# Background rounding with four raw and two high tiles, and gate and up weights loaded by depth halves

## The chip, the cores and the metric

The kernel runs on one core of a Trainium2 chip. The core has a matrix engine (TensorE, PE in the profile; its weight loads are listed as PEld), a vector engine (VectorE, DVE), an activation engine (ScalarE, ACT), a general engine (GpSimd, POOL) and a queue engine (SyncE, SP) that here only issues transfers. Data moves between the chip's memory and the on-chip memory (128 partitions) in transfers over 16 DMA engines. Each engine works through its own list of instructions in order and waits on semaphores for the others; an SP entry that has to wait therefore holds up everything behind it on SP. The metric is the device time of one execution in microseconds.

## The reference

One layer of a decoder with a sequence of 1024 rows and a model width of 1024, all in float32. Only the shape of it matters here:

```python
x = x + 0.5 * swiglu(rms_norm(x, g_ffn1), w1_gate, w1_up, w1_down)   # d_ff = 2816
h = rms_norm(x, g_mix)
proj = h @ w_in          # queries, keys, values and gates of two attention branches
...                      # sparse attention (a), stick-breaking attention (b)
x = x + merged @ w_out
x = x + 0.5 * swiglu(rms_norm(x, g_ffn2), w2_gate, w2_up, w2_down)

def swiglu(h, w_gate, w_up, w_down):
    return (silu(h @ w_gate) * (h @ w_up)) @ w_down
```

The weights `w_gate` and `w_up` are 1024 by 2816, `w_down` is 2816 by 1024. `w_in` is used in the middle of the layer, long after the first FFN.

## The kernel before

**Precision.** The matrix engine takes a rounded format. To keep float32 accuracy, each operand is split into a high part (the value rounded, written by ACT) and a low part (the value minus its high part, by POOL or DVE). A product then takes three matmuls: high by high, high by low, low by high. `halve` (L375 to L379) does such a split: ACT at L377, the subtraction at L378.

**The two FFNs.** `ffn_in` computes silu(h·gate) times (h·up) for the first FFN (tile names a...) and for the second (b...). The 2816 columns go in eleven pairs of 128-column blocks, `p`, and for each pair the gate (`e` = 0) and the up weights (`e` = 1). A pair with a depth of 1024 is a two by two matrix of blocks: A11 and A12 are the two depth halves of the first column block, A21 and A22 those of the second. From the second pair on, each of these two by two products is done with seven block products instead of eight (Strassen's scheme in Winograd's form). I call seven such products a set; there are twenty in an FFN, a gate set and an up set in turn. A product is 12 matmuls (L468 to L470: three for each of four depth chunks). The first pair is done by `opening` with eight plain block products.

Inside `products` (L477) the seven run in the order 1, 6, 7, 5, 2, 4, 3. Four PSUM letters, pa to pd, hold the results. ACT reads pa after the first product (L481), and DVE adds pb, pc and pd to running sums after the second, third and fourth (L484, L488, L491). The fifth and the seventh product go on accumulating in pa and pd, so they can start only after L481 and L491. Behind L491 DVE forms the four sums of the next set (L457 to L460, kept in program order), which ACT and POOL then split, together with the plain quarters (seven `halve` calls, L461). After an up set, DVE multiplies gate by up and forms sums of the result (L612, L589 to L592), and SP stores seven tiles to memory (L594) for the second half of the FFN, `ffn_out`, which starts at L680.

**Weights of gate and up.** `loader` (L437) loads one column block of 128 columns at full depth into a tile of 1024 floats per partition: eight runs of 128 floats, 512 bytes each. Of two such tiles the left 512 columns are A11 and A21, the right ones A12 and A22.

**Background rounding.** While the first FFN runs, the kernel also splits 24 column blocks of `w_in` (16 for the gates, eight for queries and keys), for later use, into high and low parts kept in memory. Each block goes in two pieces of 128 by 512: 48 pieces. `beside` (L784) is called after every product of the first FFN with the product's place in its set, 0 to 6. A piece takes three steps: load the raw weights (SP, L799); round them into a high tile (ACT, L789) and subtract in place, which leaves the low part in the raw tile (DVE, L790); store both (SP, L793). `behind` ties a step to the last matmul of the product, so that it cannot start earlier. There are three slots, each with one raw and one high tile. Their steps stand in `points` as (split, store, load): slot 0 at places 0, 1 and 3, slot 1 at 2, 3 and 5, slot 2 at 4, 5 and, in the next set, 0. A load goes into the tiles that its slot's store has just been reading, and at place 3 the load of slot 0 is written before the store of slot 1. The six tiles come from leftover space: c3 (three), c1 (one) and pair (two).

The order of instructions on each engine is settled at build time by a scheduler that goes by a simulated timeline, except in `opening` and where `keep_in_program_order` pins it.

Of the kernel before, what the change touches and what calls it, by code (L numbers as in the profile page):

```python
# [16 lines left out]
AF = mybir.ActivationFunctionType  # L17
ALU = mybir.AluOpType
# [5 lines left out]
P = 128  # L24
# [3 lines left out]
ND = D // P  # L28
# [29 lines left out]
def f32(ap):  # L58
    return ap.bitcast(F32)
# [186 lines left out]
def trunk(ctx, tc, x, positions, g_ffn1, w1_gate, w1_up, w1_down, g_mix, w_in, g_cq, w_uq_a, w_q_idx,  # L246
          g_q_a, g_k_a, w_uv_a, w_o_a, w_o_b, w_out, g_ffn2, w2_gate, w2_up, w2_down, inv_freq, out):
    nc = tc.nc
# [63 lines left out]
    def in_turn(*sources):  # L312

        order = [f for n in range(max(n for f, n in sources)) for f, m in sources if n < m]
        at = [0]

        def tile_(name):
            at[0] += 1
            return order[(at[0] - 1) % len(order)](name)

        return tile_
# [53 lines left out]
    def halve(t, src, eng=None):  # L375

        nc.scalar.activation(t[:, HI], src, AF.Copy)  # L377
        (eng or nc.gpsimd).tensor_tensor(t[:, LO], src, f32(t[:, HI]), op=ALU.subtract)  # L378
        return t  # L379

    class Right:


# [51 lines left out]
                nc.vector.tensor_sub(out[j], a[j], b[j])  # L435

    def loader(raw, nm):  # L437
        def load(w, f, name):
            t = raw(name)
            nc.sync.dma_start(t.rearrange("p (k f) -> p k f", k=ND),  # L440
                              w[0, :, f * P:(f + 1) * P].rearrange("(k p) f -> p k f", p=P))
            return t

        return load

    def ffn_in(nm, R, wg, wu, raw, op, sums, ct, bank, staged, rows, first=None, beside=lambda n, ins: None):

# [2 lines left out]
        B, load = R.B, loader(raw, nm)  # L450

        def left_sides(rs, name, pinned):
            A11, A12, A21, A22 = (r[:, q] for r in rs for q in (HI, LO))
            O = {n: op(f"{name}{n}") for n in ("A11", "S2", "S3", "S1", "A12", "A22", "S4")}
            s1, s2, s3, s4 = (sums(f"{name}s{n}") for n in range(1, 5))
            in_turn_ = tc.keep_in_program_order if pinned else lambda i: i
            in_turn_(nc.vector.tensor_add(s1, A21, A22))  # L457
            in_turn_(nc.vector.tensor_sub(s2, s1, A11))
            in_turn_(nc.vector.tensor_sub(s3, A11, A21))
            in_turn_(nc.vector.tensor_sub(s4, A12, s2))  # L460
            for n, src in (("A11", A11), ("S2", s2), ("S3", s3), ("S1", s1), ("A12", A12), ("A22", A22), ("S4", s4)):  # L461
                halve(O[n], src)
            return O

        def times(a, b, ps, start=True):
# [35 lines left out]
        def opening(raws, rows, nxt):  # L501


            A = [dict(zip(("A11", "A12", "A21", "A22"), (r[:, q] for r in rs for q in (HI, LO)))) for rs in raws]
            O = ({}, {})

            def left(e, *names):
                for n in names:
                    O[e][n] = halve(op(f"{nm}{e}0{n}"), A[e][n])

            ps, sg = {}, {}

            def half(e, r, c, q):

                letter = "abcd"[r + 2 * c]
                if not q:
                    ps[e, r, c] = bank(f"p{letter}", letter)
                times(O[e][f"A{r + 1}{q + 1}"], B[f"B{q + 1}{c + 1}"], ps[e, r, c], not q)

            def gate(r, c):  # L520
                sg[r, c] = ct(f"{nm}sg")
                nc.scalar.activation(sg[r, c], ps[0, r, c], AF.Silu)

            def gated(r, c):
                nc.vector.tensor_mul(sg[r, c], sg[r, c], ps[1, r, c])

            if "B11" not in B:
                left(0, "A11")
                R.operand("B12")
                R.turn("B11")  # L530
                left(0, "A12")
                R.turn("B21")
                left(0, "A21", "A22")
                R.second()
            else:
                left(0, "A11", "A12", "A21", "A22")
            for t, n in enumerate(("A11", "A12", "A21", "A22")):
                if 4 - t <= len(rows):
                    R.stat(rows[t + len(rows) - 4])
                left(1, n)  # L540
            for t in rows:
                R.norm(t)
            half(0, 0, 0, 0)
            half(0, 0, 0, 1)
            gate(0, 0)
# [12 lines left out]
            half(0, 0, 1, 0)  # L558
            R.turn("T1", "ab")
            half(0, 0, 1, 1)  # L560
            gate(0, 1)
            R.sum("T2")
            half(0, 1, 1, 0)
            R.turn("T2", "ab")
            half(0, 1, 1, 1)
            gate(1, 1)
            R.sum("T4")
            R.sum("T3")
            half(1, 0, 1, 0)
            half(1, 0, 1, 1)  # L570
            R.turn("T3", "ab")
            gated(0, 1)
            nxt = nxt()
            half(1, 1, 1, 0)
            half(1, 1, 1, 1)
            R.turn("T4", "ab")
            gated(1, 1)
            return [sg[0, 0], sg[0, 1], sg[1, 0], sg[1, 1]], [ct(f"{nm}s{n}") for n in range(3)], nxt
# [17 lines left out]
        def lefts(p, e, pinned=False):  # L596
            if p == NF // 2:
                return None
            return left_sides([load((wg, wu)[e], 2 * p + q, f"{nm}{e}r{p}") for q in range(2)], f"{nm}{e}{p}", pinned)

        for p in range(NF // 2):
            if not p:
                first = first or [[load(w, q, f"{nm}{e}r0") for q in range(2)] for e, w in enumerate((wg, wu))]
                with tc.manual_schedule(engines={e.engine for e in (nc.tensor, nc.vector, nc.scalar, nc.gpsimd)}):
                    H, S, nxt = opening(first, rows, lambda: lefts(1, 0))
            else:
                for e, w in enumerate((wg, wu)):
                    u, nxt = products(nxt, f"{nm}{e}", lambda: lefts(p + e, 1 - e, True))
                    if not e:
                        H = silu(u)  # L610
                for a, b in zip(H, u):
                    nc.vector.tensor_mul(a, a, b)  # L612
                S = u[1:]
            finish(p, H, S)
# [147 lines left out]
    with tc.tile_pool(name="ring1", bufs=1) as rpool, tc.tile_pool(name="s1", bufs=1) as spool, tc.tile_pool(name="ps1", bufs=1, space=PSUM) as psum:  # L762
# [3 lines left out]
        with tc.tile_pool(name="t1", bufs=1, side="right") as tpool, tc.tile_pool(name="c1", bufs=1) as cpool:  # L766
# [2 lines left out]

            c4, c5, c3, c1 = (of(cpool, f"c{n}", n, 512, F32R) for n in (4, 5, 3, 1))  # L770
            ct = fp(in_turn(*[(f, 1) for f in [c4] * 4 + [c5] * 5]))
            spare = in_turn((c3, 3), (c1, 1), (pair, 2))
            R = Right(g_ffn1, bank, fp(op), fp(in_turn((c5, 5), (c3, 3))), tt, "a")
            xs = []

            pieces = [(nm, c) for nm in columns for c in range(0, 1024, 512)]
            held, points = {}, ((0, 1, 3), (2, 3, 5), (4, 5, 0))

            def behind(ins, *others):
                for o in others:  # L780
# [2 lines left out]

            def beside(n, ins):  # L784

                for slot, (split_, store, load_) in enumerate(points):
                    if n == split_ and slot in held:
                        nm, c, raw, hi = held[slot]
                        behind(ins, nc.scalar.activation(hi, raw, AF.Copy))  # L789
                        nc.vector.tensor_tensor(raw, raw, f32(hi), op=ALU.subtract)  # L790
                    if n == store and slot in held:
                        nm, c, raw, hi = held.pop(slot)
                        behind(ins, *(nc.sync.dma_start(d[:, c:c + 512], part)  # L793
                                      for d, part in zip(split_of[nm], (f32(hi), raw))))
                    if n == load_ and pieces:
                        nm, c = pieces.pop(0)
                        raw, hi = f32(spare(f"swr{slot}")), spare(f"swh{slot}")
                        held[slot] = nm, c, raw, hi
                        behind(ins, nc.sync.dma_start(raw.rearrange("p (k f) -> p k f", f=P),  # L799
                                                      rows_of[:, c // P:(c + 512) // P, columns[nm]:columns[nm] + P]))  # L800

            def rows(t):
                xs.append(fp(tt)(f"x{t}"))
# [3 lines left out]
            for t in range(4):  # L807
                rows(t)
                if t == 1:
                    R.gain()  # L810
            first = [[load(w, q, f"a{e}r0") for q in range(2)] for e, w in enumerate((w1_gate, w1_up))]
            for t in range(4, NT):
                rows(t)
            gcolm = column(g_mix, ND, "gcolm")
# [9 lines left out]
                R.norm(t)  # L824
            R.second = lambda: R.place(xs[4:8], 1, sums)
            ffn_in("a", R, w1_gate, w1_up, raw, op, sums, ct, bank, staged[0], range(4), first, beside)
            assert not held and not pieces
        hpool.append(tc.tile_pool(name="hpool", bufs=1, side="right"))
        hstack = ExitStack()
        hpool[0] = hstack.enter_context(hpool[0])  # L830
# [1342 lines left out]
```

## Time and profile before

| | |
|---|---|
| median of three runs | 2239.9 us (2239.87 to 2240.59) |
| the profiled execution's own time | 2240.86 us |
| its span, first to last instruction | 2239.1 us |
| mean granted TensorE clock | 0.989 |
| PE busy | 2169.2 us (97%) |
| DVE, ACT, POOL busy | 1526.3, 1104.4, 858.2 us |
| moved by DMA | 381.01 MB, 170 GB/s on average |

The page gives busy time by engine and in 40 slices, the DMA queues, the chain of work that ended last, the costliest groups of instructions and the DMA issues with their time from issue to landing. Groups are named by line, engine, operation and tiles (out<-in). A wait is written as the engine and line that waited, an arrow, and what released it. On the page the clock row is 9 (90% or more) in every slice of 56 us; shorter windows show where it fell.

### The profile page before, as it was taken

To read this page: it belongs to the slowest core of one execution; us is meant where nothing else is said; L and a number is where in the kernel's file an instruction comes from. 1 tells how busy PE (TensorE), PEld (TensorE's weight loads), DVE (VectorE), ACT (ScalarE), POOL (GpSimd) and SP (SyncE) were. 2 spreads that over 40 slices of the span, in tenths; PEclk is the share of its full clock that TensorE was granted. 3 is DMA by queue.
4 is the path that set the end of the run, shared out by engine and by line. 5 is a ranking of instruction groups with operands and counts; after the bars stand their busy time and mean duration, and the time that the engine had idled before them with its cause. 6 is when DMAs were issued, how large, how long until landed. Compare 5 with 4: busy or idle time off the path is not lost.

```text
span 2239.1 us, 30578 instructions
## 1 busy us (share of the span) xinstructions
PE 2169.2 (97%) x10460; PEld 1807.1 (81%) x10460; DVE 1526.3 (68%) x2548; ACT 1104.4 (49%) x2169; POOL 858.2 (38%) x698
## 2 busy tenths in 40 slices
PE   7999999999999999899999899999999999999999
PEld 6887787788878988788788788877888888888877
DVE  5675675687875498677788688853465564668685
ACT  4333333334445258999989466533333232233443
POOL 3355455532236344211111322255245454552233
PEclk9999999999999999999999999999999999999999
DMA  5376676688686333665554623566223233349755
GB/s 171 99 216 199 205 239 190 195 286 275 198 219 177 111 118 126 195 176 170 151 160 164 209 95 99 170 218 236 67 77 117 90 113 97 115 160 324 229 165 184
DMA packets 269052, 381.01 MB, mean 170 GB/s; under 512 B 23264, under 2 KB 157040, under 8 KB 268896
## 3 DMA queue, kind: packets, MB, share of 16 engines
q1 hardware_dynamic: 256384, 339.17, 48.9%
q0 software_dynamic: 12512, 39.89, 4.9%
q8 instruction: 82, 1.34, 0.2%
q14 instruction: 74, 0.61, 0.1%
HBM read 259.94 MB, written 119.05 MB: 169 GB/s over the span
## 4 chain that ended last, share of the span: by engine, by line
PE 70%; ACT 7%; DVE 6%; DMA 4%; issue 3%; POOL 2%; SPq 0%; ACTq 0%; POOLq 0%; DVEq 0%
PE p L681 6%; PE p L682 6%; PE p L680 6%; ACT junka L1186 3%; PE pd L468 3%; PE pd L469 3%; PE pd L470 3%; PE pc L470 3%; PE pc L468 3%; PE pc L469 3%; PE pa L469 3%; PE pa L468 3%; PE pa L470 3%; PE psf L308 2%; PE psf L309 2%
## 5 line engine op out<-in xcount | busy, mean ns | idle before, releaser
L1186 ACT ACTIVATE junka<-u,cand,sig 128x768 bf16<-128x768 f32 (+4 forms) x186 | 183.8, 988 | 5.6 <-DVE cand L1183 4.0
L790 DVE TENSOR_TENSOR swr<-swr,swh 128x512 f32<-128x512 f32 x48 | 45.8, 954 | 111.2 <-ACT swh L789 107.2
L789 ACT ACTIVATE swh<-swr 128x512 fp32r<-128x512 f32 x48 | 30.2, 630 | 165.6 <-DMA swr<-in_w_in_dram 56.5
L1627 DVE TENSOR_TENSOR_SCAN left<-left 128x640 f32<-128x640 f32 (+3 forms) x64 | 86.3, 1349 | 4.0 <-ACT left L1619 4.0
L1120 POOL DMA_DIRECT2D gd<-evg x32 | 17.9, 560 | 152.6 <-ACT evg L1117 112.7
L1676 DVE TENSOR_TENSOR pt<-pstT,pt 128x512 fp32r<-128x512 f32 (+1 forms) x96 | 50.8, 549 | 28.6 <-ACT pt L1674 28.3
L584 ACT ACTIVATE b0u<-b0u 128x512 f32<-128x512 f32 x20 | 12.7, 633 | 95.3 <-DVE b0u L491 78.9
L1676 DVE TENSOR_TENSOR pt<-pspT,pt 128x512 fp32r<-128x512 f32 x72 | 46.8, 684 | 16.3 <-ACT pt L1674 16.3
L681 PE MATMUL p<-bT,bS 128*128 128x512 f32 x132 | 52.5, 398 | 2.4 <-DVE bT L378 2.4
L1674 ACT ACTIVATE pt<-pspT 128x512 fp32r<-128x512 f32 x72 | 39.7, 596 | 29.2 <-PE pspT L1886 29.1
L1807 ACT ACTIVATE e<-e,nm 128x256 f32<-128x256 f32 (+7 forms) x64 | 49.3, 773 | 9.3 <-DVE nm L1802 9.2
L1540 DVE SCALAR_TENSOR_TENSOR u<-relu,WI,u 128x512 f32<-128x512 f32 (+1 forms) x70 | 50.1, 733 | 5.2 <-ACT relu L1533 4.6
L1795 DVE CUSTOM_DVE_ANT_0 e<-psL,bias 128x512 f32<-128x512 f32 (+3 forms) x96 | 49.7, 550 | 5.5 <-PE psL L1832 5.5
L682 PE MATMUL p<-bT,bS 128*128 128x512 f32 x132 | 51.9, 396 | 1.0 <-POOL bS L378 1.0
L681 PE MATMUL p<-aT,aS 128*128 128x512 f32 x132 | 51.5, 390 | 0.0
L1630 DVE TENSOR_TENSOR sa<-sa,left 128x639 f32<-128x639 f32 (+3 forms) x64 | 48.1, 752 | 3.7 <-ACT sa L1621 0.2
L682 PE MATMUL p<-aT,aS 128*128 128x512 f32 x132 | 50.4, 389 | 0.0
L1674 ACT ACTIVATE pt<-pstT 128x512 fp32r<-128x512 f32 (+1 forms) x96 | 47.1, 519 | 3.3 <-PE pstT L1730 3.1
L1533 ACT ACTIVATE relu<-psdot 128x512 f32<-128x512 f32 (+1 forms) x80 | 40.1, 520 | 17.4 <-DVE u L1540 8.6
L1886 PE MATMUL pspT<-ident,e 128*128 128x128 f32 x288 | 39.6, 277 | 8.1 <-DVE ri L1809 5.5
L1619 ACT ACTIVATE left<-psz 128x512 f32<-128x512 f32 (+2 forms) x96 | 46.2, 505 | 2.0 <-PE psz L1654 1.8
L1621 ACT ACTIVATE sa<-psz 128x512 f32<-128x512 f32 (+2 forms) x96 | 47.0, 511 | 0.1
(3021 smaller groups left out, 8247.8 us busy)
## 6 DMA issues: line engine op xcount, KB each, us to landing
aw<-in_w_down_dram SPq DMA_DIRECT2D x33, 512.0 KB, 4.9
bw<-in_w_down_dram SPq DMA_DIRECT2D x33, 512.0 KB, 5.0
swr<-in_w_in_dram SPq DMA_DIRECT2D x48, 256.0 KB, 5.1
a0r<-in_w_gate_dram SPq DMA_DIRECT2D x22, 512.0 KB, 6.7
a1r<-in_w_up_dram SPq DMA_DIRECT2D x22, 512.0 KB, 7.2
b0r<-in_w_gate_dram SPq DMA_DIRECT2D x22, 512.0 KB, 4.2
b1r<-in_w_up_dram SPq DMA_DIRECT2D x22, 512.0 KB, 3.9
x<-in_x_dram SPq DMA_DIRECT2D x16, 512.0 KB, 6.1
```

The source lines that it names most:

```text
L468: nc.tensor.matmul(ps, a[:, c], b[k][:, HI], start=start and k == 0, stop=False, skip_group_check=True)
L469: nc.tensor.matmul(ps, a[:, c], b[k][:, LO], start=False, stop=False, skip_group_check=True)
L470: ins = nc.tensor.matmul(ps, a[:, l], b[k][:, HI], start=False, stop=k == 3, skip_group_check=True)
L680: nc.tensor.matmul(ps[q][m], S[:, h], T[:, HI], start=p == 0, stop=False)
L681: nc.tensor.matmul(ps[q][m], S[:, h], T[:, LO], start=False, stop=False)
L682: nc.tensor.matmul(ps[q][m], S[:, l], T[:, HI], start=False, stop=p == last)
L1186: nc.scalar.activation(junks[1][:, 0:(i + 1) * P], score[i], AF.Sign, scale=sig[:, b:b + 1], bias=cand.bitcast(F32)[:, b:b + 1], accum_out ...
L1540: nc.vector.scalar_tensor_tensor(ac, r, wv, ac, op0=ALU.mult, op1=ALU.add)
L1627: nc.vector.tensor_tensor_scan(back, back, back, 1.0, op0=ALU.mult, op1=ALU.bypass)
L1674: nc.scalar.activation(pt[:, off:512], tp[:, off:512], AF.Copy)
L1676: nc.vector.tensor_sub(pt[:, 512 + off:1024], tp[:, off:512], f32(pt[:, off:512]))
L1795: nc.vector.tensor_tensor_reduce(e[:, c], lp[:, 0:n_], bias[:, c], 1.0, LOW, op0=ALU.add, op1=ALU.max, accum_out=m)
```

## The change

Two things are changed.

First, the loads of gate and up weights, in both FFNs. A tile now holds one depth half of both column blocks: four runs of 256 floats, 1 KB each, as many bytes as before. The quarters A11 to A22 become views of four runs of 128 floats, 256 apart: A11 and A21 lie in the first tile, A12 and A22 in the second. The sums (L457 to L460) and the splits of the quarters and sums work on such views; a new function `quarter` takes the place of `halve` there. The number and size of these operations stay the same.

Second, the background rounding of the first FFN. The four c3 and c1 tiles rotate as raw tiles, the two pair tiles as high tiles. Three pieces are still rounded per set, at places 0, 2 and 4, and stored at places 1, 3 and 5, from the second set on. The load of a piece is now due three products after the rounding of the piece four before it, at places 3, 5 and 0 of the next set, into that piece's raw tile, and that is six or seven products ahead of its own rounding. Where a store and a load are due at one place, the store comes first. A high tile is written again by the second rounding after.

```diff
+    def quarter(t, src):
+        nc.scalar.activation(by_depth(t[:, HI]), src, AF.Copy)
+        nc.gpsimd.tensor_tensor(by_depth(t[:, LO]), src, by_depth(f32(t[:, HI])), op=ALU.subtract)
+        return t
...
-        def load(w, f, name):
+        def load(w, p, q, name):
             t = raw(name)
-            nc.sync.dma_start(t.rearrange("p (k f) -> p k f", k=ND),
-                              w[0, :, f * P:(f + 1) * P].rearrange("(k p) f -> p k f", p=P))
+            nc.sync.dma_start(t.rearrange("p (k f) -> p k f", k=4),
+                              w[0, q * 512:q * 512 + 512, p * 2 * P:(p + 1) * 2 * P].rearrange("(k p) f -> p k f", p=P))
             return t
...
+    def quarters(rs):
+        t = [r.rearrange("p (k m f) -> p m k f", k=4, m=2) for r in rs]
+        return [t[q][:, m] for m in range(2) for q in range(2)]
+
+    def by_depth(a):
+        return a.rearrange("p (k f) -> p k f", k=4)
...
-            A11, A12, A21, A22 = (r[:, q] for r in rs for q in (HI, LO))
+            A11, A12, A21, A22 = quarters(rs)
...
-            spare = in_turn((c3, 3), (c1, 1), (pair, 2))
+            early, late = fp(in_turn((c3, 3), (c1, 1))), pair
...
-            held, points = {}, ((0, 1, 3), (2, 3, 5), (4, 5, 0))
+            splits = [7 * (k // 3 + 1) + (0, 2, 4)[k % 3] for k in range(len(pieces))]
+            agenda, held, halved, turn = defaultdict(list), [], [], [0]
+            for k, n in enumerate(splits):
+                agenda[n].append("split")
+                agenda[n + 1].append("store")
+                agenda[splits[k - 4] + 3 if k > 3 else k].append("load")
...
             def beside(n, ins):
+                at, turn[0] = turn[0], turn[0] + 1
+                for step in agenda.pop(at, ()):
+                    if step == "load":
+                        nm, c = pieces.pop(0)
+                        raw = early("swr")
+                        held.append((nm, c, raw))
+                        behind(ins, nc.sync.dma_start(raw.rearrange("p (k f) -> p k f", f=P),
+                                                      rows_of[:, c // P:(c + 512) // P, columns[nm]:columns[nm] + P]))
+                    elif step == "split":
+                        nm, c, raw = held.pop(0)
+                        hi = late("swh")
                         behind(ins, nc.scalar.activation(hi, raw, AF.Copy))
                         nc.vector.tensor_tensor(raw, raw, f32(hi), op=ALU.subtract)
+                        halved.append((nm, c, raw, hi))
+                    else:
+                        nm, c, raw, hi = halved.pop(0)
                         behind(ins, *(nc.sync.dma_start(d[:, c:c + 512], part)
                                       for d, part in zip(split_of[nm], (f32(hi), raw))))
```

More of the change, by code (lines that the diff above doesn't have):

```diff
@@ L452, in left_sides @@
         def left_sides(rs, name, pinned):
-            A11, A12, A21, A22 = (r[:, q] for r in rs for q in (HI, LO))
+            A11, A12, A21, A22 = quarters(rs)
             O = {n: op(f"{name}{n}") for n in ("A11", "S2", "S3", "S1", "A12", "A22", "S4")}
-            s1, s2, s3, s4 = (sums(f"{name}s{n}") for n in range(1, 5))
+            s1, s2, s3, s4 = (by_depth(sums(f"{name}s{n}")) for n in range(1, 5))
             in_turn_ = tc.keep_in_program_order if pinned else lambda i: i
@@ L461, in left_sides @@
             for n, src in (("A11", A11), ("S2", s2), ("S3", s3), ("S1", s1), ("A12", A12), ("A22", A22), ("S4", s4)):
-                halve(O[n], src)
+                quarter(O[n], src)
             return O
@@ L501, in opening @@
         def opening(raws, rows, nxt):
-            A = [dict(zip(("A11", "A12", "A21", "A22"), (r[:, q] for r in rs for q in (HI, LO)))) for rs in raws]
+            A = [dict(zip(("A11", "A12", "A21", "A22"), quarters(rs))) for rs in raws]
             O = ({}, {})
@@ L508, in left @@
                 for n in names:
-                    O[e][n] = halve(op(f"{nm}{e}0{n}"), A[e][n])
+                    O[e][n] = quarter(op(f"{nm}{e}0{n}"), A[e][n])
             ps, sg = {}, {}
@@ L598, in lefts @@
                 return None
-            return left_sides([load((wg, wu)[e], 2 * p + q, f"{nm}{e}r{p}") for q in range(2)], f"{nm}{e}{p}", pinned)
+            return left_sides([load((wg, wu)[e], p, q, f"{nm}{e}r{p}") for q in range(2)], f"{nm}{e}{p}", pinned)
         for p in range(NF // 2):
             if not p:
-                first = first or [[load(w, q, f"{nm}{e}r0") for q in range(2)] for e, w in enumerate((wg, wu))]
+                first = first or [[load(w, 0, q, f"{nm}{e}r0") for q in range(2)] for e, w in enumerate((wg, wu))]
                 with tc.manual_schedule(engines={e.engine for e in (nc.tensor, nc.vector, nc.scalar, nc.gpsimd)}):
@@ L784, in beside @@
             def beside(n, ins):
-                for slot, (split_, store, load_) in enumerate(points):
-                    if n == split_ and slot in held:
-                        nm, c, raw, hi = held[slot]
+                at, turn[0] = turn[0], turn[0] + 1
[9 more added lines that the diff above has]
+                        hi = late("swh")
                         behind(ins, nc.scalar.activation(hi, raw, AF.Copy))
                         nc.vector.tensor_tensor(raw, raw, f32(hi), op=ALU.subtract)
-                    if n == store and slot in held:
-                        nm, c, raw, hi = held.pop(slot)
+                        halved.append((nm, c, raw, hi))
+                    else:
+                        nm, c, raw, hi = halved.pop(0)
                         behind(ins, *(nc.sync.dma_start(d[:, c:c + 512], part)
                                       for d, part in zip(split_of[nm], (f32(hi), raw))))
[L795 to L800, printed above, removed]
             def rows(t):
@@ L810, in trunk @@
                     R.gain()
-            first = [[load(w, q, f"a{e}r0") for q in range(2)] for e, w in enumerate((w1_gate, w1_up))]
+            first = [[load(w, 0, q, f"a{e}r0") for q in range(2)] for e, w in enumerate((w1_gate, w1_up))]
             for t in range(4, NT):
@@ L826, in trunk @@
             ffn_in("a", R, w1_gate, w1_up, raw, op, sums, ct, bank, staged[0], range(4), first, beside)
-            assert not held and not pieces
+            assert not agenda and not held and not halved and not pieces
         hpool.append(tc.tile_pool(name="hpool", bufs=1, side="right"))
```

## The prediction

> **What bounds the kernel now.** I read the page first, then the busy time of two stretches that run the same matmuls, then the waits, the chain and SyncE's queue (SP) inside the slower one.
>
> The page's first rows: the span, and the busy time of TensorE (PE) with its share and instructions.
>
> ```profile
> span 2239.1 us, 30578 instructions
> PE 2169.2 (97%) x10460; PEld 1807.1 (81%) x10460; DVE 1526.3 (68%) x2548; ACT 1104.4 (49%) x2169; POOL 858.2 (38%) x698
> ```
>
> Only 70 us of the span are without a matmul, so a gain must come from a place where PE waits. The products of the first FFN (gate and up, tiles a...) and of the second (b...) are the same code. The first rows of each tile's and line's view give their starts; the windows view gives the stretches between, with busy time (and count) of each engine, then clock, DMA share and GB/s.
>
> ```profile
> L468 PE MATMUL pc<-aT,a01S x4: 389/392/478, 75.3 to 77.9; 128*128 128x512 f32 x4
> L468 PE MATMUL pc<-bT,b01S x4: 389/389/476, 1639.0 to 1641.6; 128*128 128x512 f32 x4
> L680 PE MATMUL p<-aT,aS x132: 388/389/395, 478.4 to 654.9; 128*128 128x512 f32 x132
> L680 PE MATMUL p<-bT,bS x132: 388/389/402, 2020.2 to 2201.9; 128*128 128x512 f32 x132
> 75.30:478.40 403.10, 389.26 (x1682) 318.96 (x1681) 262.34 (x325) 140.12 (x254) 211.15 (x140) 0.98 0.69 205
> 1639.00:2020.20 381.20, 381.20 (x1683) 315.30 (x1682) 225.83 (x275) 114.43 (x206) 200.79 (x140) 1.00 0.36 116
> ```
>
> The second FFN's PE is busy all 381.20 us: 1683 matmuls at 0.2265 us, so a product of 12 takes 2.72 us and a set of seven 19.04. The first FFN takes 403.10 for the same work: **21.9 us lost**, 13.84 of them idle (403.10 − 389.26), the other 8.06 a lower clock after the idle time. The losses stand in a few places; two of the 19 us slices (columns as above):
>
> ```profile
> 212.00:231.00 19.00, 15.69 (x62) 12.50 (x61) 4.67 (x6) 5.36 (x10) 7.87 (x7) 0.91 0.51 133
> 345.00:364.00 19.00, 14.62 (x53) 11.51 (x52) 7.93 (x12) 4.79 (x9) 4.77 (x4) 0.82 0.57 140
> ```
>
> Who waited for whom up to the end of the first FFN's products (total, times, longest; the PE rows from the window 0 to 560, the others from 75 to 480):
>
> ```profile
> PE pd L468 <- DVE a1u L491: 9.9, 4, 4.4
> PE pa L468 <- ACT a1u L481: 3.3, 1, 3.3
> DVE swr L790 <- ACT swh L789: 107.2, 30, 9.1
> ACT swh L789 <- DMA swr<-in_w_in_dram: 56.5, 20, 7.2
> ```
>
> L789 and L790 are the background rounding. PE waits for evictions (L481, L491) that are queued on ScalarE (ACT) and VectorE (DVE) behind a rounding whose weights have not landed. The chain around the worst stall (start, length, what) shows why they are late:
>
> ```profile
> 217.63 8.11 DMA wg0ld<-swr
> ...
> 225.82 0.38 SPq L799
> ...
> 227.80 6.08 DMA a1r<-in_w_up_dram
> ...
> 234.01 0.64 ACT swh L789
> ...
> 235.28 0.69 DVE a1u L491
> ...
> 236.01 0.51 PE pd L468
> ```
>
> A store of rounded weights takes 8.1 us to land; SP, which issues in order, waits for it before the load into the same tile. SP's queue, and the next PE row after product four of an undisturbed set:
>
> ```profile
> 207.61 0.71 SPq L793 DMA_DIRECT2D wg0ld<-swr  x1
> 216.28 0.38 SPq L799 DMA_DIRECT2D swr<-in_w_in_dram  x1
> 216.77 0.44 SPq L793 DMA_DIRECT2D wg0hd<-swh  x1
> 217.63 0.32 SPq L793 DMA_DIRECT2D wg0ld<-swr  x1
> 225.82 0.38 SPq L799 DMA_DIRECT2D swr<-in_w_in_dram  x1
> ...
> 289.45 0.39 PE L468 MATMUL pa<-aB,a06A 128*128 128x512 f32 x1
> ...
> 299.72 0.38 SPq L799 DMA_DIRECT2D swr<-in_w_in_dram  x1
> ```
>
> Store, wait, load, next store, wait, load: a chain with one landing in each link. The load due when the fourth product ended (289.45) went out at 299.72, 10 us late, in a set without a stall. So SP is always behind, and PE stops when one landing is longer than usual.
>
> **The change, part by part.** Landing times of 256 KB stores (median from issue), of 512 KB loads and of the second FFN's stores:
>
> ```profile
> wg8hd<-swh SPq DMA_DIRECT2D x2, 256.0 KB, 11.0
> wg12ld<-swr SPq DMA_DIRECT2D x2, 256.0 KB, 5.4
> wg0ld<-swr SPq DMA_DIRECT2D x2, 256.0 KB, 8.4
> b0r<-in_w_gate_dram SPq DMA_DIRECT2D x18, 512.0 KB, 4.2
> bw<-in_w_down_dram SPq DMA_DIRECT2D x11, 512.0 KB, 4.6
> staged<-b0u SPq DMA_DIRECT2D x19, 256.0 KB, 2.0
> ```
>
> *Order of stores and loads.* Before, at the fourth and sixth product of a set the load comes first, and the store that is due there queues behind that load's wait. After, the store comes first and the load waits for a store two products older. Three landings per set in series (3 × 5.4 = 16.2 us, and 25.2 at 8.4) shrink, with SP on time, to what two products (5.44 us) don't cover: 0 at 5.4, 3 us each at 8.4. The stores and loads themselves are as many as before.
>
> *Lead of the load.* Before, a piece is rounded four products (10.9 us) after its load is due, after the change six or seven (16.3 to 19.0). With the 10 us of lateness and a median landing of 5.1 us (page, part 6) the old data come 4.2 us after their rounding is due; the new ones 1.2 to 3.9 us before it, even if SP stays as late. That is the term: the waits behind L789, and with them the 21.9 us.
>
> *Two high tiles.* This is the new wait: a high tile is written again four or five products after the rounding before it (10.9 or 13.6 us), so its store must have landed. From issue one product later this leaves 8.2 us in the tightest case, against 5.4. In the sets that follow an up set, SP's store also stands behind the staged stores, which wait for L592:
>
> ```profile
> 289.48 0.68 DVE L592 TENSOR_TENSOR a0u<-a0c,a1c 128x512 f32<-128x512 f32 x1
> ```
>
> That set began at 278.57 (289.45 less four products), so the first store there leaves at about +12.3 and lands at +17.7, while the third rounding is due at +13.6: ACT waits some 4.1 us, before the remaining halves of the next set's operands. What covers it: a PE eviction behind a rounding is needed three products (8.2 us) after it was due, less about 2.6 us of ACT, DVE and semaphore time: 5.5 us. So nothing is lost at 5.4 us landing; at 8.4 it would be 1.6 us.
>
> *Views.* Rounding and sums now read four runs of 128 with a stride. The nearest rows for such operands, a flat one beside each:
>
> ```profile
> L1432 DVE TENSOR_TENSOR kt<-KK,rope x2: 680/686/692, 765.9 to 776.8; 128x512 f32<-128x512 f32 x2
> L491 DVE TENSOR_TENSOR b0u<-b0u,pd x10: 686/687/689, 1651.7 to 1992.9; 128x512 f32<-128x512 f32 x10
> L378 POOL TENSOR_TENSOR b06S<-b06s,b06S x4: 1297/1648/1741, 1824.8 to 1832.2; 128x512 fp32r<-128x512 f32 x4
> L1025 POOL TENSOR_TENSOR wqil<-wqir,wqih x1: 2402/2402/2402, 763.3 to 763.3; 128x1024 fp32r<-128x1024 f32 x1
> POOL b11S L378 <- ACT b11S L377: 8.2, 1, 8.2
> ```
>
> L1432 reads runs of 64 with a stride and costs what L491 does: 0 on DVE, and I take 0 on ACT too. For GpSimd (POOL) no row has it. Lower end 0 (the elements are as many); upper end: its fixed part, 2 × 1.297 − 2.402 = 0.19 us, three times more for each operation, 0.58 × 7 = 4.0 us a set. POOL sits idle 8.2 us before a set's first operation, so both ends cost nothing; without that cover it would be up to 4.0 × 40 sets. I take 0, by the DVE row.
>
> *Runs of 1 KB.* At 512 KB the 512-byte runs land in 4.2 us, the long runs of `bw` in 4.6: no gain to be had per load, and their consumer (L457) comes over 20 us after the issue. 0, bounds ±0.5 for the opening, where the second depth half is now needed for A12. The first sum needs both tiles instead of one; both loads are issued together, so 0. In the second FFN, PE is full: 0.
>
> **Sum.** −21.9, +1.5 that I leave for one short stall while the first pieces fill (its store, `wg8hd`, took 11.0): −20.4. The profiled execution took 2240.9 (span 2239.1), the median is 2239.9: **2219.5 us**.
>
> One rule speaks against this. The Trainium skill, page "DMA: Bandwidth & Descriptors", section "Anatomy of one DMA — SWDGE (gpsimd) path", has a fit of about 2 us plus bytes over 436 GB/s, which for 256 KB is an estimate of 2.6 us. By it a store would land within two products, SP would not fall behind, and this change would save nothing; it is the third rival. The trace differs on this queue: 2.0 us only in the quiet second FFN, 5.4 to 8.4 here, and the measurement decides.
>
> **Rivals.** (1) Part of it stays: eight of the sixteen sets with rounding follow an up set. With the 8.4 us landing each loses 1.6 us and some 0.6 as much again by the clock (8.06/13.84), 2.5 in all; if that landing comes in half of them and as often again at the start of the others, 8 × 1.3 = 10 us stay: 2229.5. For it: `wg0ld`. Against: the 5.4 of `wg12ld`. (2) Slower: with two high tiles, two roundings cannot be closer than one round of ACT 0.63, DVE up to 1.77, SP about 1 and a landing. Three roundings per set need 1.5 rounds; this passes 19.04 us once a landing exceeds 9.3. At the 11.0 of `wg8hd` it is 21.6, 2.6 us a set over 16 sets: +41 − 21.9 gives 2259. For it, that row; against, the 5.4 and 8.4 of the later pieces shown. (3) No change: if stores landed within two products (2.0 us as in `staged<-b0u`), SP's chain would not be the cause, and PE would be short of DMA bandwidth, which the change leaves as it is: 2239.9. Against: the row below shows PE full while DMA moves far more.
>
> ```profile
> 500.00:540.00 40.00, 40.00 (x178) 33.14 (x177) 29.85 (x41) 19.71 (x34) 11.56 (x9) 1.00 0.91 320
> ```
>
> **How the numbers follow.** Forecast 0.70 (2216 to 2225 by itself), rival (1) 0.14, (2) 0.08, (3) 0.05, a reordering by the scheduler that I can't price 0.03, split between faster and slower. A difference of 0.2% (4.5 us) is about what can be told from none. Faster: 0.70 + 0.14 + 0.02 = 0.86; same 0.05; slower 0.09. The range reaches from the full gain with a better opening (2215) over rival (1) to 2234.
>
> **What would show it.** In the profile after: the stretch between the first a01S product and L680 near 383 us, PE busy throughout; L789's waits for `swr` loads gone or short, some for stores of the high part in their place; loads on SP within 3 us of their product. POOL's L378 at 1.3 to 1.75 would confirm the views. Wrong, if the stretch stays above 395 us, if L378 passes 2.72 us, or if the 20 us come back in a later stage.

## The result and the profile after

The changed kernel takes **2218.4 us** (median of four runs, 2217.72 to 2218.97) against 2239.9 before (now of four runs too, with the same median): a ratio of 0.9905, 95% interval 0.989 to 0.992. Predicted were 2219.5 us, with a range of 2215 to 2234. The profiled execution took 2217.72 us.

The first rows of the page of the kernel after, as shown of before:

```profile
span 2215.9 us, 30577 instructions
PE 2160.4 (97%) x10460; PEld 1803.5 (81%) x10460; DVE 1528.3 (69%) x2548; ACT 1104.4 (50%) x2169; POOL 857.3 (39%) x698
```

The same work, 23.2 us less span. PE's own busy time fell by 8.8 us, the clock's share of the old loss. Where the rest came from is told by the stretches between the same matmuls. First the tile view of the kernel after (the first and last start stand behind the durations), where L481 and L693 are the former L468 and L680:

```profile
L481 PE MATMUL pc<-aT,a01S x4: 389/389/476, 75.3 to 77.9; 128*128 128x512 f32 x4
L693 PE MATMUL p<-aT,aS x132: 389/389/393, 456.2 to 632.4; 128*128 128x512 f32 x132
L481 PE MATMUL pc<-bT,b01S x4: 389/389/476, 1617.0 to 1619.6; 128*128 128x512 f32 x4
L693 PE MATMUL p<-bT,bS x132: 388/389/402, 1997.9 to 2178.7; 128*128 128x512 f32 x132
```

Then the windows view of the kernel after between these starts, and the two slices that showed the losses before (columns as in the prediction):

```profile
75.30:456.20 380.90, 380.90 (x1683) 315.55 (x1682) 263.37 (x324) 140.66 (x254) 209.74 (x140) 1.00 0.72 215
456.20:1617.00 1160.80, 1127.24 (x5858) 947.52 (x5857) 837.46 (x1679) 723.24 (x1488) 359.66 (x353) 0.99 0.53 169
1617.00:1998.00 381.00, 381.00 (x1684) 315.61 (x1682) 226.46 (x277) 114.57 (x206) 200.72 (x140) 1.00 0.36 117
1998.00:2215.90 217.90, 210.41 (x925) 172.94 (x923) 154.71 (x197) 89.86 (x158) 66.13 (x42) 1.00 0.67 223
212.00:231.00 19.00, 19.00 (x86) 15.73 (x85) 13.06 (x17) 6.12 (x12) 9.04 (x6) 1.00 0.73 211
345.00:364.00 19.00, 19.00 (x86) 15.73 (x85) 13.68 (x17) 7.04 (x13) 9.68 (x7) 1.00 0.79 254
```

The first FFN's products are down from 403.10 to 380.90 us, with PE busy all the time and the clock at 1.00: −22.2. Before, the other three stretches were 1160.6 (1639.0 − 478.4), 381.20 and 218.9 (2239.1 − 2020.2), so they give +0.2, −0.2 and −1.0. The sum is the −23.2 of the spans. All but 1.0 us of the gain stands in the stretch that the prediction named, and none is given back later.

The waits of the kernel after (PE from the window 0 to 560, the others from 75 to 480; L815 and L816 are the rounding, formerly L789 and L790):

```profile
PE pst L433 <- DVE ay L420: 13.8, 4, 8.6
PE pst L433 <- DVE x L420: 0.6, 1, 0.6
DVE swr L816 <- ACT swh L815: 44.0, 22, 4.2
ACT swh L815 <- DMA swr<-in_w_in_dram: 9.2, 2, 7.8
ACT swh L815 <- DMA wg0hd<-swh: 5.8, 1, 5.8
ACT swh L815 <- DMA wqk10321hd<-swh: 4.8, 1, 4.8
ACT swh L815 <- DMA wqk5202hd<-swh: 4.6, 1, 4.6
```

PE's two rows are those of the opening; no product waits for an eviction any more. ACT waits for a raw load twice instead of 20 times. In place of these it waits nine times for a store of the high part, 21.8 us in all (the three longest are shown), and no product of PE waits for it.

### The profile page after: what moved, and what is told of

It reads as the page before. It is cut to its first block, busy times and chain, and to the rows that moved or that the text cites. A ratio compares the mean times of both kernels' runs of the same rounds, so it can differ in the third digit from the quotient of the medians.

```text
span 2215.9 us, 30577 instructions
## 1 busy us (share of the span) xinstructions
PE 2160.4 (97%) x10460; PEld 1803.5 (81%) x10460; DVE 1528.3 (69%) x2548; ACT 1104.4 (50%) x2169; POOL 857.3 (39%) x698
## 2 busy tenths in 40 slices
DMA packets 223997, 381.02 MB, mean 172 GB/s; under 512 B 23264, under 2 KB 111984, under 8 KB 223840
## 4 chain that ended last, share of the span: by engine, by line
PE 81%; ACT 7%; DVE 6%; issue 2%; DMA 2%; POOL 1%; SPq 0%; ACTq 0%; POOLq 0%; DVEq 0%
PE p L694 6%; PE p L695 6%; PE p L693 6%; PE pd L483 4%; PE pd L481 4%; PE pd L482 4%; PE pc L482 4%; PE pc L483 4%; PE pc L481 4%; ACT junka L1207 4%; PE pa L483 3%; PE pa L482 3%; PE pa L481 3%; PE psf L308 2%; PE psf L309 2%
## 5 line engine op out<-in xcount | busy, mean ns | idle before, releaser
L815 ACT ACTIVATE swh<-swr 128x512 fp32r<-128x512 f32 x48 | 30.2, 629 | 119.2 <-PE pc L483 47.2
L816 DVE TENSOR_TENSOR swr<-swr,swh 128x512 f32<-128x512 f32 x48 | 44.0, 916 | 48.3 <-ACT swh L815 44.0
L597 ACT ACTIVATE b0u<-b0u 128x512 f32<-128x512 f32 x20 | 12.6, 632 | 95.3 <-DVE b0u L504 78.9
```

## Experiments

The column "products" is the stretch measured above (first a01S product to the first aT, aS matmul) in each run's own profile. The column "pace" is the time from the first to the last load of a background piece, over the 47 steps between them. PE at full speed needs a piece every 6.35 us (19.04 over three). Products and pace are those of one execution; the times of one kernel spread by 1 to 11 us (e12 the most). The kernel before lies at 2236 to 2246 us over all these runs.

| run | time us | ratio, 95% interval | products us | pace us |
|---|---|---|---|---|
| before | 2239.9 | 1 | 403.1 | 6.91 |
| after | 2218.4 | 0.989 to 0.992 | 380.9 | 6.31 |
| e1 depth-half loads alone | 2225.4 | 0.9914 to 0.9953 | 387.6 | 6.58 |
| e2 new rounding alone | 2216.1 | 0.9872 to 0.9915 | 380.9 | 6.25 |
| e3 before, stores ahead of loads | 2220.3 | 0.9885 to 0.9922 | 380.9 | 6.33 |
| e4 after, loads ahead of stores | 2237.9 | 0.9979 to 0.9997 | 401.3 | 6.86 |
| e5 depth halves, 512-byte runs | 2229.4 | 0.9937 to 0.9971 | 390.5 | 6.64 |
| e6 after, one high tile | 2244.6 | 1.0015 to 1.0035 | 408.1 | 6.84 |
| e7 after, lead of four products | 2219.7 | 0.9899 to 0.9929 | 381.0 | 6.46 |
| e8 e4 with three high tiles | 2232.8 | 0.9958 to 0.9980 | 394.7 | 6.84 |
| e9 after once more | 2217.6 | 0.9886 to 0.9916 | 380.9 | 6.26 |
| e10 e2 once more | 2216.9 | 0.9879 to 0.9912 | 380.9 | 6.24 |
| e11 after, three high tiles | 2221.6 | 0.9909 to 0.9939 | 380.9 | 6.25 |
| e12 e1, both halves loaded together | 2233.4 | 0.9964 to 0.9988 | 396.8 | 6.74 |

### The two halves of the change by themselves

e1 is the kernel before with the depth-half loads and their views, and the old rounding:

```diff
-            A11, A12, A21, A22 = (r[:, q] for r in rs for q in (HI, LO))
+            A11, A12, A21, A22 = quarters(rs)
...
             held, points = {}, ((0, 1, 3), (2, 3, 5), (4, 5, 0))
```

e2 is the kernel before with the new rounding, and the old loads:

```diff
             A11, A12, A21, A22 = (r[:, q] for r in rs for q in (HI, LO))
...
-            held, points = {}, ((0, 1, 3), (2, 3, 5), (4, 5, 0))
+            splits = [7 * (k // 3 + 1) + (0, 2, 4)[k % 3] for k in range(len(pieces))]
```

> The kernel before with only the depth-half loads (runs of 1 KB, quarters as views), in both FFNs; the background rounding keeps its three slots. Theory: SyncE's chain of store, landing, load is what stops TensorE, and run length does not touch it: the first FFN's products stay near 403 us, time 2240 within 3 us. Rival (the longer runs carry the gain, by earlier landings and a freer SyncE queue): products under 392 us, time 2219 to 2230.

> The kernel before with only the new rounding (four raw and two high tiles, stores ahead of loads, six or seven products of lead); gate and up weights still in runs of 512 bytes. Theory: all of the gain is here: products near 381 us, time 2218.5 within 1.5 us. Rival (the loads do part of it): 2223 to 2240.

e2 has the whole gain; its 2216.1 us lie even 0.9 below the range expected. So the rounding suffices, as the prediction said. But e1 alone is worth 15.5 us of the products (403.1 − 387.6), where the prediction and e1's own theory had put the loads at nothing. It comes out in the range of e1's rival, though for the most part not by the rival's cause, the longer runs (e5 below). The two don't add up: they take away the same loss. e9 and e10 set the new rounding with and without the depth halves side by side again:

> The changed kernel once more, unaltered, for the comparison with the new rounding on the old loads on one chip. 2216 to 2220 us.

> The new rounding on the old loads once more. If the depth halves add nothing once the stores go ahead of the loads, it stands within 0.2% (4.4 us) of the changed kernel of the same call: 2212 to 2224 us. If the halves cost or gain something of their own there, the two differ by more, with the sign of it.

2217.6 and 2216.9, their ranges overlapping (2216.35 to 2219.9 and 2215.85 to 2218.09): beside the new rounding the depth halves make no difference that can be measured, and no run here clearly beats the changed kernel.

### Order or lead

The prediction gave the gain to the longer lead of the loads ("that is the term"). The rival is the order in SP's queue. e3 keeps the old slots, tiles and lead of the kernel before and only issues a store ahead of a load that falls on the same product:

```diff
                 for slot, (split_, store, load_) in enumerate(points):
-                    if n == split_ and slot in held:
-                        ...
                     if n == store and slot in held:
                         ...
+                for slot, (split_, store, load_) in enumerate(points):
+                    if n == split_ and slot in held:
+                        ...
                     if n == load_ and pieces:
```

> The kernel before with one edit: where a store and a load are due at the same product, the store is issued first. Three slots, tiles and four products of lead stay. If the order alone breaks the chain: loads within 3 us of their product, data landed some 5 us later against 10.9 of lead, products 381 to 386 us, time 2218 to 2223. If the lead is what counts: products above 393 us, time 2230 to 2240.

The order alone brings the products to 380.9 (456.5 − 75.6):

```profile
L468 PE MATMUL pc<-aT,a01S x4: 389/392/478, 75.6 to 78.2; 128*128 128x512 f32 x4
L680 PE MATMUL p<-aT,aS x132: 389/389/389, 456.5 to 632.7; 128*128 128x512 f32 x132
```

Nothing else was moved by this edit: in the traces of e3 and of the kernel before, PE, DVE, ACT and POOL carry out the same operations on the same tiles in the same order, and SP's transfers other than the background's stand in the same order too. So the reordering by the scheduler that the prediction allowed for is not the cause. The same comparison holds for e7 and e4 against the kernel after. e7 tests the same from the other side: the changed kernel with the load due four products ahead of its rounding, as before the change.

```diff
-                agenda[splits[k - 4] + 3 if k > 3 else k].append("load")
+                agenda[splits[k] - 4].append("load")
```

> The changed kernel with one edit: a load is due four products before its rounding, as in the kernel before, not six or seven. Two high tiles, stores ahead of loads; a load now finds its tile's store five or six products old. If the order of SyncE's queue is what the gain hangs on: no stall, 2217 to 2221. If the longer lead is needed: waits for the raw loads come back, products above 388 us, time above 2225.

Nothing is lost: 381.0. And e4 keeps the long lead and puts the load ahead of the store again:

```diff
             agenda, held, halved, turn = defaultdict(list), [], [], [0]
+            for k in range(len(splits)):
+                agenda[splits[k - 4] + 3 if k > 3 else k].append("load")
             for k, n in enumerate(splits):
                 agenda[n].append("split")
                 agenda[n + 1].append("store")
-                agenda[splits[k - 4] + 3 if k > 3 else k].append("load")
```

> The changed kernel with one edit: at a product where both are due, the load is issued ahead of the store, as before. Four raw and two high tiles and the longer lead stay. If the lead alone covers SyncE's lateness: 2218 to 2221. If the order counts: SyncE stays some 10 us late, a store lands about 18 us after its rounding while the high tile is due again after 10.9 or 13.6, ScalarE waits 5 to 7 us a set against 5.5 of cover, and up to 2.5 us a set is lost: 2225 to 2258.

With the lead but without the order, 20.4 of the 22.2 us are lost again. In e4, though, what ACT waits for are now mostly stores of the high tiles, so two high tiles could have been to blame and the lead have worked without them. e8 gives e4 a third high tile (a buffer of the sums, which keep four), and e11 is its counterpart with the change's own order:

```diff
-        sums, pair = of(spool, "s", 5, 512), of(spool, "pair", 2, 512, F32R)
+        sums, pair, s5 = of(spool, "s", 4, 512), of(spool, "pair", 2, 512, F32R), of(spool, "s5", 1, 512, F32R)
...
-            early, late = fp(in_turn((c3, 3), (c1, 1))), pair
+            early, late = fp(in_turn((c3, 3), (c1, 1))), in_turn((pair, 2), (s5, 1))
```

> The changed kernel with the load put ahead of the store in SP's queue, as in the run that took 2237.9 us with the products at 401.3 us, and now with four raw and three high tiles; the third high tile takes one sum buffer's memory. If the longer lead of the load covers SP's lateness, and only the two high tiles kept it from doing so, the products come to 381 to 386 us and the time to 2217 to 2222. If it is the load standing ahead of the store in one queue that costs, whatever number of high tiles there is, the products stay at 394 us or more and the time at 2230 or more. In between, both have a share.

> The changed kernel in its own order (store ahead of load) with three high tiles, the third from a sum buffer: what the run with the load first and three high tiles (2232.8 us, products 394.7) is to be read against. If the sum buffer that was given up costs nothing, this stands at the changed kernel's 2217.6 us within 4 us, with the products at 380 to 383 us, and the 13.7 us by which that run was slower are the order's. If the sum buffer is what cost, this is at 2225 or more.

e8 comes out as the second theory had it, just above its bound of 394. Compared with e4, the third high tile is worth 6.6 us (401.3 − 394.7). With the same tiles, the order is worth 13.8 (394.7 − 380.9). e11's total is 4 us above the changed kernel of e9, and not in the products: the first and the last start of the next stage's matmuls (p<-aT,aS) are 181.5 us apart in e11 (456.2 to 637.7) and 176.5 in e9. With the buffers exchanged the scheduler orders that stage's matmuls in another way; its cost was not traced further.

Why the longer lead did not make up for the order in e4 and e8 is shown by the loads of the background pieces in the tile view, first and last start. Before:

```profile
L799 SPq DMA_DIRECT2D swr<-in_w_in_dram x48: 368/384/7028, 81.0 to 406.0; - x48
```

e4 and e8, loads first:

```profile
L811 SPq DMA_DIRECT2D swr<-in_w_in_dram x48: 383/384/2650, 85.0 to 407.5; - x48
```

```profile
L811 SPq DMA_DIRECT2D swr<-in_w_in_dram x48: 383/384/2619, 85.5 to 407.2; - x48
```

e3 and the kernel after, stores first:

```profile
L800 SPq DMA_DIRECT2D swr<-in_w_in_dram x48: 367/420/6803, 81.3 to 378.7; - x48
```

```profile
L810 SPq DMA_DIRECT2D swr<-in_w_in_dram x48: 367/386/2095, 84.9 to 381.3; - x48
```

In these three runs with the load first, the 48th load leaves at 406 to 407.5 us: the chain store, landing, load runs at a pace of 6.84 to 6.91 us a piece, and PE wants one every 6.35. The difference of 0.49 to 0.56 us over 47 pieces is 23 to 26 us. A lead or another tile is a stock: it lets PE run ahead of the chain once, by some products, and is then used up. With the store first, the pace is PE's own (6.24 to 6.33; 6.46 in e7, whose first load leaves 3.8 us earlier than that of the kernel after and whose last leaves 3.2 later).

This is no rule for every kernel with the load first. e1 has it first too, with a lead of four, and its last load leaves at 390.3:

```profile
L812 SPq DMA_DIRECT2D swr<-in_w_in_dram x48: 368/384/817, 81.2 to 390.3; - x48
```

The chains differ in length. SP's own waits (window 75 to 480; the rows of the background load's line that name a store of a low part, added up) have 30 of the 48 loads waiting for a store in the kernel before and 30 in e1, which is two of the three in a set; in e4 and e8 it is 44. So with the load first, the four raw tiles put a third landing per set in series. e4 and e8 therefore do not test the longer lead by itself on the old chain, and no run does. That the lead is not needed, and that it does not replace the order in the changed kernel, is what e3, e7 and e4 show. With the stores first, the same rows count 14 loads in e3, 20 in the kernel after and none in e7: in e7 the store that a load waits for has come due five or six products earlier, in the kernel after only two.

The same is seen in one set, gate pair 6, in the timelines. A set starts with a06A; its stores are due 5.44, 10.88 and 16.32 us later (two, four and six products). The kernel after:

```profile
265.84 0.39 PE L481 MATMUL pa<-aB,a06A 128*128 128x512 f32 x1
...
273.61 0.68 DVE L605 TENSOR_TENSOR a0u<-a0c,a1c 128x512 f32<-128x512 f32 x1
...
274.74 0.37 SPq L820 DMA_DIRECT2D wg5hd<-swh  x1
...
276.95 0.32 SPq L820 DMA_DIRECT2D wg6hd<-swh  x1
...
279.19 0.38 SPq L810 DMA_DIRECT2D swr<-in_w_in_dram  x1
...
282.39 0.34 SPq L820 DMA_DIRECT2D wg6hd<-swh  x1
...
283.30 0.44 SPq L810 DMA_DIRECT2D swr<-in_w_in_dram  x1
```

Due at 271.28, 276.72 and 282.16, the stores leave 3.5, 0.2 and 0.2 us late, the loads behind them 2.5 and 1.1. In e4 and e8 the same set and stores:

```profile
274.85 0.39 PE L481 MATMUL pa<-aB,a06A 128*128 128x512 f32 x1
...
288.81 0.46 SPq L821 DMA_DIRECT2D wg5hd<-swh  x1
...
296.71 0.69 SPq L821 DMA_DIRECT2D wg6hd<-swh  x1
```

```profile
267.06 0.39 PE L481 MATMUL pa<-aB,a06A 128*128 128x512 f32 x1
...
288.77 0.44 SPq L821 DMA_DIRECT2D wg5hd<-swh  x1
...
295.90 0.46 SPq L821 DMA_DIRECT2D wg6hd<-swh  x1
```

SP is 8.5 and 11.0 us late in e4, 16.3 and 18.0 in e8 (from 280.29 and 285.73; 272.50 and 277.94). The third high tile lets PE start the set 7.8 us earlier and leaves the stores where they were.

### What the depth halves did

e5 has the depth halves of e1, each tile loaded by two transfers of 256 KB in 512-byte runs, so that only the run length differs.

```diff
-            nc.sync.dma_start(t.rearrange("p (k f) -> p k f", k=4),
-                              w[0, q * 512:q * 512 + 512, p * 2 * P:(p + 1) * 2 * P].rearrange("(k p) f -> p k f", p=P))
+            for m in range(2):
+                nc.sync.dma_start(t.rearrange("p (k m f) -> p m k f", k=4, m=2)[:, m],
+                                  w[0, q * 512:q * 512 + 512, (2 * p + m) * P:(2 * p + m + 1) * P].rearrange("(k p) f -> p k f", p=P))
```

> The depth-half loads alone (the kernel before in its rounding), but each half is loaded by two transfers of 256 KB with runs of 512 bytes instead of one of 512 KB with runs of 1 KB. The first tile of a pair is still free early, so its load still goes out apart from the second tile's. If the gain of the depth halves comes from that early release, which splits the 1 MB burst ahead of a background load: products 384 to 393 us, time 2220 to 2230. If it comes from the 1 KB runs: products above 396, time 2233 to 2241.

It keeps 12.6 of e1's 15.5 us (403.1 − 390.5), so the runs are not the main thing. Their 2.9 us are not settled: the times of e1 and e5 overlap. What else the depth halves alter is when a tile comes free: A11 and A21, now both in the first tile, are read early, A12 and A22 late, where before each tile held a late one. e12 undoes only this: e1 with the load of the first half made to wait for the last quarter read from the second half.

```diff
+                if n == "A22":
+                    ends.append(quarter.last)
...
+                rs.append(load((wg, wu)[e], p, q, f"{nm}{e}r{p}"))
+                if nm == "a" and not q and len(ends) > 1:
+                    tc.add_manual_dep(load.last.ins, ends[-2].ins.name, mybir.DependencyInfo(
+                        mybir.DependencyClass.Sync, mybir.DependencyReason.DATA), reason="pace")
```

> The kernel before with the weights loaded by depth halves alone (2225.4 us, products 387.6 us), and the load of a pair's first half held back until its second half's tile is free too, so that both go out together as before the change. If the depth halves won because the two loads go out apart, each into a tile as it comes free, this falls back to 398 us or more for the products and 2234 or more in time. If they won by the longer runs or the fewer packets, it stays at 386 to 391 us and 2223 to 2229.

SP's queue between 205 and 240 us has two loads of a1r; in e1, in e12 and, third, in the kernel before:

```profile
210.81 0.40 SPq L446 DMA_DIRECT2D a1r<-in_w_up_dram  x1
218.69 0.38 SPq L812 DMA_DIRECT2D swr<-in_w_in_dram  x1
...
220.15 0.47 SPq L446 DMA_DIRECT2D a1r<-in_w_up_dram  x1
220.72 0.64 SPq L812 DMA_DIRECT2D swr<-in_w_in_dram  x1
```

```profile
222.09 1.16 SPq L446 DMA_DIRECT2D a1r<-in_w_up_dram  x2
223.35 1.30 SPq L820 DMA_DIRECT2D swr<-in_w_in_dram  x1
224.74 3.61 SPq L814 DMA_DIRECT2D wg1hd<-swh  x1
```

```profile
227.32 1.33 SPq L440 DMA_DIRECT2D a1r<-in_w_up_dram  x2
228.75 5.05 SPq L799 DMA_DIRECT2D swr<-in_w_in_dram  x1
```

In e1 they leave 9.3 us apart; in e12, as before the change, both go out within 1.3 us, 1 MB at once. e12 gives back 9.2 of the 15.5 us (396.8 − 387.6; by the medians of the time 8.0 of 14.9). It missed its own bounds of 398 and 2234, so this is the larger share and not the whole. The paces go along with it: 6.91 before, 6.74 in e12, 6.64 in e5, 6.58 in e1, and 47 × (6.91 − 6.58) = 15.5. But a load is tied to a product, so a PE that is held up slows the loads too, and the agreement alone does not tell which drives which. The depth halves helped only while the loads stood ahead of the stores; once the stores go first SP isn't what PE waits for, and nothing is left for them to gain.

What they shorten in SP's queue is not settled. It is not the number of landings in series: 30 loads wait for a store before, in e1 and in e12. Nor is it their length, which was my reading: these waits add up to 134.5 us before, 144.4 in e1 and 153.8 in e12. What the rows do show is the issue itself. Behind the two loads of the kernel before, the next background load takes 5.05 us to go out; in e12 that load and the store behind it take 1.30 and 3.61; in e1 no background load takes more than 0.82 (its row above; before, up to 7.03). Whether that is the whole of the 9.2 us no run measured.

### One high tile

e6 makes the feared wait worse: five raw tiles and one high one.

```diff
-            early, late = fp(in_turn((c3, 3), (c1, 1))), pair
+            early, late = fp(in_turn((c3, 3), (pair, 2))), c1
```

> The changed kernel with one high tile (c1) and five raw tiles in place of two and four. Each rounding must now wait until the store of the rounding before has landed. By the formula of the prediction's slower rival, three roundings per set need three rounds of ScalarE 0.63, VectorE 0.7 to 1.8, SyncE about 1 and a landing of 5.4: 23 to 26 us against 19.04, 4 to 7 us a set over 16 sets: 2282 to 2330. If the cover of 5.5 us is enough, or the rounds overlap: 2218 to 2225.

The waits of e6, and the background loads in its tile view:

```profile
PE pd L481 <- DVE a0u L504: 12.9, 6, 4.0
ACT swh L815 <- DMA wg15hd<-swh: 15.6, 2, 12.0
```

```profile
L810 SPq DMA_DIRECT2D swr<-in_w_in_dram x48: 368/444/2947, 85.4 to 407.0; - x48
```

The mechanism is real: ACT waits for stores of the high part, and PE for evictions behind it. It is slower than before, but by less than forecast (2244.6 us against 2282 to 2330). With one high tile I take the pace of 6.84 us for the mean round; 16 sets of 3 × 6.84 − 19.04 give 23.7 us against the 27.2 measured (408.1 − 380.9). The prediction's round (ACT 0.63, DVE up to 1.77, SP 1, landing 5.4) came to 8.8. Without DVE it is 7.0: the store of the high part does not wait for DVE's subtraction, which only reads that tile, and can leave once ACT has written it. At 6.84 a round, an estimate for two high tiles is 10.3 us of a set's 19.04.

## Why the prediction was right, and where it was not

*The bound and its place: right.* SP's chain of store, landing and load made the rounding late, and evictions queued behind it; e3 changes only the order in SP's queue and the 22.2 us are there. The worth of the stretch (21.9, idle and clock together) came back in full: in the two slices the clock went from 0.91 and 0.82 to 1.00.

*Lead of the load: wrong as the term.* "The new ones 1.2 to 3.9 us before it, even if SP stays as late. That is the term" failed. It took SP's lateness for a constant. e4 and e8 show a rate instead: a chain 0.5 us too slow per piece, so that with six or seven products of lead 20.4 (e4) and 13.8 us (e8, which has a third high tile besides) of the 22.2 stay lost. And e7 loses nothing with the old lead. The time came out right in spite of this because the change holds the order too; that part is luck.

*Order of stores and loads: the term, under-rated.* The prediction described it rightly (landings in series shrink to what two products don't cover) but gave it no worth of its own. It is worth 22.2 us on the old tiles, 20.4 on the new. Of the three landings per set that it puts in series before the change, the trace has two (30 of 48 loads); what was said of the slots ahead of the prediction, that a load goes where its slot's store has just been reading, does not show as a wait for the third.

*Two high tiles: 0, right, by other sizes than I gave.* The store after an up set left at +8.9 us (274.74 − 265.84) and not at +12.3, because the subtraction L605 that the staged stores wait for comes at +7.8 now; before, the same subtraction (L592) came at +10.9 (289.48 − 278.57). ACT waited nine times, at most 5.8 us, near the cover of 5.5.

*Views: 0, right.* POOL's split and DVE's sum of the kernel after, on the strided views of the raw tiles:

```profile
L384 POOL TENSOR_TENSOR a00A<-a0r,a00A x4: 1262/1288/1301, 13.2 to 23.1; 128x512 fp32r<-128x512 f32 x4
...
L470 DVE TENSOR_TENSOR a11s<-a1r,a1r x1: 685/685/685, 88.6 to 88.6; 128x512 f32<-128x512 f32 x1
```

The POOL splits of a00A take 1.262 to 1.301 us, against 1.263 to 1.299 for the same ones on flat runs before (L378); the upper end of 0.58 us more does not exist here. DVE's 0.685 is that of L491.

*Depth-half loads: 0 beside the new rounding, right; 0 by themselves, wrong.* The step looked for their effect in the landing of a single load. The larger share lay in the moment at which a tile comes free, and so in what SP sends out back to back (e12).

*The 1.5 us left for a short stall: not there.* No product waits at all, which is why the stretch gained 22.2 and not 20.4.

*The rivals.* (1), part stays: no; the 8.4 us landings are still there (8.6 for `wg0ld` below) and cost nothing. (2), the high tiles as the limit: a true mechanism with too dear a round (e6). (3), stores that land within two products: no. Landings in the window 75 to 480 of the kernel after:

```profile
swr<-in_w_in_dram SPq DMA_DIRECT2D x48, 256.0 KB, 6.4
wg12ld<-swr SPq DMA_DIRECT2D x2, 256.0 KB, 4.6
wg15ld<-swr SPq DMA_DIRECT2D x2, 256.0 KB, 5.7
wg0ld<-swr SPq DMA_DIRECT2D x2, 256.0 KB, 8.6
```

The estimate of 2.6 us worked out from the Trainium skill, page "DMA: Bandwidth & Descriptors", section "Anatomy of one DMA — SWDGE (gpsimd) path", is off by two to three times here, where the transfers go out on SP and not by the path of that section, as the trace before had already said.

*What was to show it.* Stretch near 383: 380.9. L789's waits for `swr` gone or short: 56.5 us in 20 down to 9.2 in 2. Loads within 3 us of their product: 2.5 and 1.1 in the set shown. POOL's split at 1.3 to 1.75 us: yes. One of these signs is weaker than I took it for. e3, without a stall of PE in the products, has ACT waiting for raw loads longer than the kernel before did (its waits, 75 to 480):

```profile
ACT swh L794 <- DMA swr<-in_w_in_dram: 69.6, 18, 9.3
```

Such a row counts how long ACT stood with nothing else to do, and not how late an eviction became. The pace of the loads against PE's is the better sign.

## What to carry to other kernels

Where a queue that issues in order carries both the store that empties a buffer and the load that refills it, first ask what stands between a store coming due and its issue: a load that waits ahead of it puts its landing in series with the next, and swapping the two lines was worth all of this change. Compare the pace of such a chain with the pace at which the consumer asks: against a chain that is slower by a little every step, more lead and a further buffer helped only for a time here (e4 and e8). And where data are cut over two buffers, put what is read early into one and what is read late into the other, so that each refill goes out as its buffer comes free; here that was worth 9.2 us (e12 against e1) while the queue was late, and nothing that can be told once it was not.

## What the runs showed that I had not expected

Landings did not shorten when the stalls went. The median of the 48 background loads rose from 5.1 to 6.4 us, with 215 instead of 205 GB/s in the stretch: so the gain comes from what waits for what, and not from faster transfers.

Loading by depth halves cut the DMA packets from 269052 to 223997 for the same bytes, and beside the new rounding this changed no time that can be told (e9 and e10).
